# Raw weight tiles of the FFN in two sets of slots, with loads up to nine tiles ahead

## The chip, the cores and the metric

The kernel runs on one core of a Trainium2 chip. The metric is the time of one execution on the device, in microseconds (us). The engines are TensorE (PE in the profile; PEld is its weight load), VectorE (DVE), ScalarE (ACT), GpSimd (POOL) and SyncE (SP), which only issues DMAs here. Each takes its instructions from a queue of its own, in order, and waits on semaphores for the others.

## The reference

Two layers of an encoder trunk on x of 512 positions by 1024 channels, in float32. Each layer has two attention mixers (A: sparse, with an indexer and top-k; B: latent) with gates and projections, and then a channel mixer. The change sits in the weights of the channel mixer, called the FFN below:

```python
h = rms_norm(x, norm_ffn[l])
u = causal_dwconv(h @ w_up[l], conv_w[l], conv_b[l])      # w_up: 1024 x 5632, width 3
val, gat = u[..., :D_FF], u[..., D_FF:]                   # D_FF = 2816
x = x + (jax.nn.silu(gat) * val) @ w_down[l]              # w_down: 2816 x 1024
```

## The kernel before

All products are float32 made from three products of a shorter type: each operand is split in a high part (a cast on ScalarE) and a low part (the difference), and TensorE adds high by high, high by low and low by high.

The class `Weights` streams the weights from HBM as a list of tiles, 148 per layer, in the order in which TensorE uses them. The numbers of tiles below count from the start of layer 0. Tiles 0 to 59 belong to the mixers, the gates and the projections. The FFN has two parts. Part 1: up tiles `uv0`, `ug0` to `uv9`, `ug9` (value and gate columns; tiles 60 to 79), then 20 down tiles `dn` (80 to 99). Part 2: `uv10` to `ug21` (100 to 123), then 24 `dn` tiles (124 to 147). Layer 1 repeats this, 148 later.

A tile goes through these steps:

- `load` (L156): SP loads the raw tile `wr` (512 KB; 256 KB for `dn`). `wr` has four slots.
- `split` (L173, L191 for `dn`): ScalarE casts it to the high part `wh`.
- The low part `wl`: for `uv` and `ug`, `low_by_dma` lets ScalarE write the negated high part (L201), and POOL issues a DMA that adds the raw tile into it (L202). This accumulate DMA reads `wr`, so the slot is free when it has landed. For `dn`, VectorE subtracts (L196); so it does (L185) for an up tile right behind a `dn` tile.
- Before the split of a `dn` tile, `sums` (L213, L214, L215) makes its 4 blocks into 7 in place, for a product scheme with 7 products instead of 8. For the first four `dn` tiles of a part all three run on POOL; later, in part 1, L213 and L214 on VectorE and L215 on POOL; in part 2, L213 on VectorE and the others on POOL.

TensorE calls `get` for a tile. After its matmuls `ahead` runs: it splits the next three tiles and loads up to the sixth. Each up tile is 24 matmuls of 512 columns. Behind each up tile comes a conv: ScalarE L1365, then VectorE L1368 and L1369 from TensorE's bank; for a `ug` tile then silu (L357) and the product (L1386), and after every second pair `act_pair`, which makes the operands of the down tiles: L1342 to L1345, and the splits `b11`, `b21`, `t1`, `t3` (high parts on ScalarE, low parts at L303). A down tile is 21 matmuls of 256 columns (L1424), of which the first six read `b11`, `t1` and `t3`. The last three tiles of the kernel use `last_products` (L1495 to L1497).

Mixer A has pair tiles `P` of 128 x 1280, with three slots of their own (L1093, read by the transposes at L1052); they are not used in the FFN. The program is written in this order, and a list scheduler then sets each engine's queue.

Of the kernel before, what the change touches and what calls it, by code (L numbers as in the profile page):

```python
# [10 lines left out]
F32 = mybir.dt.float32  # L11
# [69 lines left out]
WMOD = 1  # L81
NEWT = 1
WB = [4, 4, 3]
N_SLOTS = 65
FS = 10
DNV = 1
# [42 lines left out]
W_COLS = max(n for _, _, n in PLAN)  # L129


class Weights:
# [18 lines left out]
    def load(self, i):  # L151
        if i >= len(self.seq) or i in self.raw:
            return
        n = self.seq[i][2]
        t = self.pool.tile([128, W_COLS], F32, name=f"wr{i}", tag="wr", bufs=WB[0])
        self.nc.sync.dma_start(t[:, :n], self.source(i, 0, n))  # L156
        self.raw[i] = t

    def split(self, i, lag=0):
# [4 lines left out]
        t = self.raw[i]  # L164
        h = self.pool.tile([128, W_COLS], F32R, name=f"wh{i}", tag="wh", bufs=WB[1])
        o = self.pool.tile([128, W_COLS], F32R, name=f"wl{i}", tag="wl", bufs=WB[1])
        name = self.seq[i][0]
# [36 lines left out]
    def sums(self, i, t):  # L204
# [3 lines left out]
        su = SU2 if self.seq[i][1] % 11 >= FS // 2 else SUMS  # L208
        if self.seq[i - WB[1]][0] != "dn":
            su = "012"  # L210
# [13 lines left out]
    def ahead(self):  # L224

        for j in range(1, WB[1]):
            self.split(self.at + j, 2)
        for j in range(WB[1], WB[1] + WB[0] - 1):
            self.load(self.at + j)
        if PRE and self.at + WB[1] < len(self.seq) and self.seq[self.at + WB[1]][0] == "dn":  # L230
            self.sums(self.at + WB[1], self.raw[self.at + WB[1]])
# [3 lines left out]
def trunk(ctx: ExitStack, tc: tile.TileContext, xT, wd, vecs, bias, rot_n, outT):  # L235
# [8 lines left out]
    def nm(s):  # L244
        uid[0] += 1
        return f"{s}_{uid[0]}"

    def slot(s, dt=F32):
        return sb.tile([128, 512], dt, name=nm(s), tag="slot", bufs=N_SLOTS)

# [118 lines left out]
    x0 = [slot("x") for _ in range(KD)]  # L369
    warm = sb.tile([128, 512], BF, name="warm", tag="slot", bufs=N_SLOTS)  # L370
    V.memset(warm, 0.0)
# [1257 lines left out]
```

## Time and profile before

| | |
|---|---|
| median of 3 runs (lowest to highest) | 1539.27 us (1538.85 to 1540.74) |
| profiled execution, and its span | 1542.47 us, 1540.8 us |
| granted clock | 1.00 |
| TensorE, TensorE's weight load | 1528.9 us (99%), 1337.1 us (87%) |
| VectorE, ScalarE, GpSimd | 1124.0 us (73%), 945.9 us (61%), 395.0 us (26%) |
| HBM | 141.06 MB read, 94 GB/s over the span |

The busy times are of one execution, and each row in the views names the engine, the line of the kernel, the tile that is written and those that are read. In the views of waits, an entry says who waited, at which line, for whom, and then the total in us, how often, and the longest. `SPq` is a load that waits in SP's queue for its slot.

### The profile page before, as it was taken

To read this page: it belongs to the slowest core of one execution; us is meant where nothing else is said; L and a number is where in the kernel's file an instruction comes from. 1 tells how busy PE (TensorE), PEld (TensorE's weight loads), DVE (VectorE), ACT (ScalarE), POOL (GpSimd) and SP (SyncE) were. 2 spreads that over 40 slices of the span, in tenths; PEclk is the share of its full clock that TensorE was granted. 3 is DMA by queue.
4 is the path that set the end of the run, shared out by engine and by line. 5 is a ranking of instruction groups with operands and counts; after the bars stand their busy time and mean duration, and the time that the engine had idled before them with its cause. 6 is when DMAs were issued, how large, how long until landed. Compare 5 with 4: busy or idle time off the path is not lost.

```text
span 1540.8 us, 23967 instructions
## 1 busy us (share of the span) xinstructions
PE 1528.9 (99%) x8666; PEld 1337.1 (87%) x8666; DVE 1124.0 (73%) x2303; ACT 945.9 (61%) x1553; POOL 395.0 (26%) x578
## 2 busy tenths in 40 slices
PE   9999999999999999999999999999999999999998
PEld 8887999888888898889998889998888888988898
DVE  7899988666476693547979999885574857845577
ACT  7756677773577536665557677686635765456642
POOL 2343012300012331125502520223001115311355
PEclk9999999999999999999999999999999999999999
DMA  7464124733478448873554641356435783588723
GB/s 245 104 160 122 46 92 110 186 120 119 127 189 190 103 117 219 191 178 96 151 165 112 166 99 56 103 135 173 131 99 144 177 190 95 152 197 195 176 77 109
DMA packets 73575, 216.29 MB, mean 140 GB/s; under 512 B 8432, under 2 KB 11504, under 8 KB 73456
## 3 DMA queue, kind: packets, MB, share of 16 engines
q1 hardware_dynamic: 54592, 149.08, 31.0%
q0 software_dynamic: 18432, 65.28, 22.6%
q8 instruction: 68, 1.11, 0.3%
q14 instruction: 51, 0.42, 0.1%
q10 hardware_dynamic: 432, 0.40, 0.1%
HBM read 141.06 MB, written 4.19 MB: 94 GB/s over the span
## 4 chain that ended last, share of the span: by engine, by line
PE 82%; DVE 12%; ACT 3%; issue 1%; POOL 0%; DMA 0%; DVEq 0%; ACTq 0%
PE D L516 35%; PE T L516 15%; PE D L539 6%; PE L L1424 5%; PE T L1424 4%; PE D L1424 3%; DVE sc L1021 2%; PE Y L1059 2%; DVE m L1014 2%; PE Y L1424 2%; PE T L1052 2%; PE L L516 2%; PE L L324 1%; PE L L323 1%; PE L L706 1%
## 5 line engine op out<-in xcount | busy, mean ns | idle before, releaser
L173 ACT CAST wh<-wr 128x1024 fp32r<-128x1024 f32 (+2 forms) x205 | 211.2, 1033 | 164.4 <-PE D L516 73.5
L202 POOL DMA_DIRECT2D wl<-wr x128 | 110.8, 877 | 633.0 <-ACT wl L201 604.4
L516 PE MATMUL D<-hxh,wh 128*128 128x512 f32 (+1 forms) x440 | 174.2, 396 | 0.0
L516 PE MATMUL D<-hxl,wh 128*128 128x512 f32 (+1 forms) x440 | 172.9, 393 | 0.0
L201 ACT ACTIVATE wl<-wr 128x1024 fp32r<-128x1024 f32 (+2 forms) x128 | 132.2, 1035 | 47.9 <-PE D L516 25.7
L191 ACT CAST wh<-wr 128x896 fp32r<-128x896 f32 x88 | 82.7, 941 | 103.8 <-POOL wr L215 69.6
L1093 POOL TENSOR_TENSOR P<-M,sel 128x128 f32<-128x128 f32 (+1 forms) x64 | 54.5, 907 | 272.9 <-DMA M<-in_bias_dram 239.3
L516 PE MATMUL D<-hxh,wl 128*128 128x512 f32 (+1 forms) x440 | 117.9, 393 | 0.0
L539 PE MATMUL D<-wh,hxh 128*128 128x256 f32 x384 | 113.8, 297 | 0.0
L196 DVE TENSOR_TENSOR wl<-wr,wh 128x896 fp32r<-128x896 f32 x88 | 103.8, 1181 | 8.2 <-ACT wh L191 3.1
L215 POOL TENSOR_TENSOR wr<-wr 128x256 f32<-128x256 f32 x88 | 93.8, 1068 | 60.8 <-DVE wr L214 48.3
L539 PE MATMUL D<-wl,hxh 128*128 128x256 f32 x384 | 109.3, 285 | 0.0
L539 PE MATMUL D<-wh,hxl 128*128 128x256 f32 x384 | 108.4, 283 | 0.0
L185 DVE TENSOR_TENSOR wl<-wr,wh 128x1024 fp32r<-128x1024 f32 x77 | 95.4, 1245 | 6.6 <-ACT wh L173 5.6
L516 PE MATMUL D<-hrl,wh 128*128 128x512 f32 x256 | 99.6, 389 | 0.0
L516 PE MATMUL D<-hrh,wh 128*128 128x512 f32 x256 | 99.6, 389 | 0.0
L516 PE MATMUL T<-hrh,wh 128*128 128x512 f32 x256 | 99.6, 389 | 0.0
L516 PE MATMUL T<-hrl,wh 128*128 128x512 f32 x256 | 99.6, 389 | 0.0
L516 PEld LDWEIGHTS D<-hxh,wh 128*128 128x128 f32 x440 | 82.9, 188 | 13.4 <-DVE gb L680 0.2
L516 PEld LDWEIGHTS D<-hxl,wh 128*128 128x128 f32 x440 | 82.9, 188 | 12.7
L516 PEld LDWEIGHTS D<-hxh,wl 128*128 128x128 f32 x440 | 80.2, 188 | 14.0
L1368 DVE SCALAR_TENSOR_TENSOR c<-T,vec,c 128x511 f32<-128x511 f32 x32 | 23.9, 748 | 89.1 <-ACT c L1365 89.1
(454 smaller groups left out, 4577.2 us busy)
## 6 DMA issues: line engine op xcount, KB each, us to landing
wr<-in_wd_dram SPq DMA_DIRECT2D x197, 512.0 KB, 3.7
wl<-wr POOLq DMA_DIRECT2D x120, 512.0 KB, 5.3
wr<-in_wd_dram SPq DMA_DIRECT2D x88, 256.0 KB, 2.6
x<-in_xT_dram SPq DMA_DIRECT2D x16, 256.0 KB, 4.8
M<-in_bias_dram SPq DMA_DIRECT2D x16, 256.0 KB, 4.0
wr<-in_wd_dram SPq DMA_DIRECT2D x7, 384.0 KB, 3.3
kah<-kah SPq DMA_DIRECT2D x16, 128.0 KB, 4.5
kal<-kal SPq DMA_DIRECT2D x16, 128.0 KB, 3.7
```

The costliest lines, as they stand in the source:

```text
L173: ins = self.nc.scalar.copy(h[:, :n], t[:, :n])
L185: eng.tensor_tensor(out=o[:, c], in0=t[:, c], in1=h[:, c].bitcast(F32), op=OP.subtract)
L191: self.nc.scalar.copy(h[:, :896], t[:, 128:1024])
L196: self.later(lag, lambda: self.nc.vector.tensor_tensor(out=o[:, :896], in0=t[:, 128:1024], in1=h[:, :896].bitcast(F32), op=OP.subtract))
L201: self.nc.scalar.activation(o, t, AF.Copy, scale=-1.0)
L202: self.nc.gpsimd.dma_start(o.bitcast(F32), t, accum_op=OP.add)
L215: g(2)(out=b[:, 6:8], in0=b[:, 0:3:2], in1=b[:, 3:6:2], op=OP.add)
L516: mm(p[:, t0:], lhsT=w, rhs=x[:, t0:], start=n == 0, stop=n == len(seq) - 1, skip_group_check=True)
L539: mm(pp[b][:, t, :], lhsT=x, rhs=w, start=n == 0 and half == 0 and t == 0, stop=n == 11 and half == 1, skip_group_check=True)
L1014: ins = V.max(out=m8[i], in_=st["sc"][i][:, :128 * (i + 1)])
L1093: G.tensor_tensor(out=P[:, P0[i]:P0[i] + w], in0=M[:, 512 - w:512], in1=sel[:, SEL0[i]:SEL0[i] + w], op=OP.add)
L1424: mm(p, lhsT=w, rhs=x, start=b0, stop=b1, skip_group_check=True)
```

## The change

FFN tiles whose number leaves 1, 3 or 5 when divided by 7 are loaded into the three slots of mixer A's pair tiles (tag `P`), the others into the four slots of `wr`. In the FFN a raw slot is so used again by the tile seven later, where it was four. `ahead` loads up to the ninth tile instead of the sixth, as far as these are FFN tiles. Splits still look three tiles ahead; the `sums` of a `dn` tile four ahead are still asked for at the end of `ahead`. Lines below the first edit move by 3 to 5 in `Weights` (L156 is L161 after, L202 is L207, L213 is L218), and by 7 behind it (L1368 is L1375, L1424 is L1431).

```diff
--- before.py
+++ after.py
@@ -81,6 +81,8 @@
 WMOD = 1
 NEWT = 1
 WB = [4, 4, 3]
+FFN = ('uv', 'ug', 'dn')
+SPARE = (1, 3, 5)
 N_SLOTS = 65
 FS = 10
 DNV = 1
@@ -151,8 +153,11 @@
     def load(self, i):
         if i >= len(self.seq) or i in self.raw:
             return
-        n = self.seq[i][2]
-        t = self.pool.tile([128, W_COLS], F32, name=f"wr{i}", tag="wr", bufs=WB[0])
+        name, _, n, _ = self.seq[i]
+        if name in FFN and i % (WB[0] + WB[2]) in SPARE:
+            t = self.pool.tile([128, 1280], F32, name=f"wr{i}", tag="P", bufs=WB[2])
+        else:
+            t = self.pool.tile([128, W_COLS], F32, name=f"wr{i}", tag="wr", bufs=WB[0])
         self.nc.sync.dma_start(t[:, :n], self.source(i, 0, n))
         self.raw[i] = t
 
@@ -225,7 +230,9 @@
 
         for j in range(1, WB[1]):
             self.split(self.at + j, 2)
-        for j in range(WB[1], WB[1] + WB[0] - 1):
+        for j in range(WB[1], WB[1] + WB[0] - 1 + WB[2]):
+            if j >= WB[1] + WB[0] - 1 and not (self.at + j < len(self.seq) and self.seq[self.at + j][0] in FFN):
+                break
             self.load(self.at + j)
         if PRE and self.at + WB[1] < len(self.seq) and self.seq[self.at + WB[1]][0] == "dn":
             self.sums(self.at + WB[1], self.raw[self.at + WB[1]])
```

TensorE's queue is the same in both. The queues of VectorE and POOL differ near the ends of the up tiles and in the down tiles. In the two fences that follow, from POOL at the end of layer 0's part 1, `t` is `act_pair`'s first subtract (L1342, L1349 after), and the rows of 128x1024 are accumulate DMAs. Before, `wl_5490`, `wl_5550`, `wl_5586`, `wl_5624` belong to tiles 75, 76, 77, 78 (`ug7`, `uv8`, `ug8`, `uv9`), and `wr_5590`, `wr_5628` to tiles 80, 81:

```order
L1342 TENSOR_TENSOR t_5512<-c_5420 128x256
L202 DMA wl_5490<-wr_5380 128x1024
L202 DMA wl_5550<-wr_5418 128x1024
L202 DMA wl_5586<-wr_5458 128x1024
L213 TENSOR_TENSOR wr_5590<-wr_5590 128x128
L214 TENSOR_TENSOR wr_5590<-wr_5590 128x128
L215 TENSOR_TENSOR wr_5590<-wr_5590 128x256
L202 DMA wl_5624<-wr_5494 128x1024
L213 TENSOR_TENSOR wr_5628<-wr_5628 128x128
L214 TENSOR_TENSOR wr_5628<-wr_5628 128x128
L215 TENSOR_TENSOR wr_5628<-wr_5628 128x256
L1342 TENSOR_TENSOR t_5685<-c_5592 128x256
```

After, the same accumulates write `wl_5496`, `wl_5556`, `wl_5592`, `wl_5630`, and `wr_5464`, `wr_5500`, `wr_5560`, `wr_5596` are tiles 80 to 83:

```order
L207 DMA wl_5496<-wr_5230 128x1024
L218 TENSOR_TENSOR wr_5500<-wr_5500 128x128
L219 TENSOR_TENSOR wr_5500<-wr_5500 128x128
L220 TENSOR_TENSOR wr_5500<-wr_5500 128x256
L218 TENSOR_TENSOR wr_5560<-wr_5560 128x128
L219 TENSOR_TENSOR wr_5560<-wr_5560 128x128
L220 TENSOR_TENSOR wr_5560<-wr_5560 128x256
L207 DMA wl_5556<-wr_5276 128x1024
L207 DMA wl_5592<-wr_5320 128x1024
L218 TENSOR_TENSOR wr_5596<-wr_5596 128x128
L219 TENSOR_TENSOR wr_5596<-wr_5596 128x128
L220 TENSOR_TENSOR wr_5596<-wr_5596 128x256
```

The sums of 80 (just above these rows), 81 and 82 have moved ahead of accumulate 76, and those of 83 ahead of accumulate 78.

VectorE at the same place, before: `c<-D` is the conv of `uv7`, `c<-T` that of `ug7`, and L1386 the product of the two:

```order
L303 TENSOR_TENSOR b11l_5519<-c_5592,b11h_5518 128x256
L1368 SCALAR_TENSOR_TENSOR c_5630<-D_5594,vec,c_5630 128x511
L1369 SCALAR_TENSOR_TENSOR c_5630<-D_5594,vec,c_5630 128x510
L1368 SCALAR_TENSOR_TENSOR c_5669<-T_5632,vec,c_5669 128x511
L1369 SCALAR_TENSOR_TENSOR c_5669<-T_5632,vec,c_5669 128x510
L1386 TENSOR_TENSOR c_5669<-c_5669,c_5630 128x512
```

After, `wr_5634` is tile 84 and `wr_5670` tile 85:

```order
L310 TENSOR_TENSOR b11l_5525<-c_5598,b11h_5524 128x256
L218 TENSOR_TENSOR wr_5634<-wr_5634 128x128
L1375 SCALAR_TENSOR_TENSOR c_5636<-D_5600,vec,c_5636 128x511
L219 TENSOR_TENSOR wr_5634<-wr_5634 128x128
L1376 SCALAR_TENSOR_TENSOR c_5636<-D_5600,vec,c_5636 128x510
L218 TENSOR_TENSOR wr_5670<-wr_5670 128x128
L1375 SCALAR_TENSOR_TENSOR c_5675<-T_5638,vec,c_5675 128x511
L219 TENSOR_TENSOR wr_5670<-wr_5670 128x128
L1376 SCALAR_TENSOR_TENSOR c_5675<-T_5638,vec,c_5675 128x510
L1393 TENSOR_TENSOR c_5675<-c_5675,c_5636 128x512
```

The first two sums of tiles 84 and 85 (L218, L219), which before stood behind the convs of `uv8` and `ug8`, now stand ahead of and between those of `uv7` and `ug7`.

## The prediction

> **What bounds the kernel now.** I read the page first, then the list of waits, then TensorE's chain.
>
> ```profile
> PE 1528.9 (99%) x8666; PEld 1337.1 (87%) x8666; DVE 1124.0 (73%) x2303; ACT 945.9 (61%) x1553; POOL 395.0 (26%) x578
> ...
> PE D L1497 <- DVE wl L196: 1.5, 1, 1.5
> PE T L376 <- DVE warm L371: 1.2, 1, 1.2
> ...
> SPq L156 <- DMA wl<-wr: 745.1, 128, 14.9
> ...
> 508.95 5.44 PE D L516 x24
> ...
> 538.26 0.72 PE D L1424 x6
> ...
> 540.78 0.98 PE D L1424 x6
> ```
>
> TensorE is busy for 99% of the span, and its order does not change. In the FFN the list shows one wait of it, the 1.5 us at the kernel's end. SP's weight loads do wait, 745.1 us in total behind the accumulate DMAs that free a raw slot, but no TensorE wait follows from that: more raw slots remove a wait that costs nothing. So the question is how the new order of the other queues changes the times at which TensorE gets its operands. The last two rows show where nothing is spare: the first down tiles of layer 0's part 1 (TensorE goes over from `ug9` to `dn` at 530.7). Six matmuls take 0.72 us elsewhere and 0.98 us at 540.78. They read `b11h`, `b11l`, `t1h`, `t1l`, `t3h`, `t3l`, and `t3l` is the last thing that VectorE writes before them:
>
> ```profile
> 510.74 0.75 DVE L1368 SCALAR_TENSOR_TENSOR c<-T,vec,c 128x511 f32<-128x511 f32 x1 [3.90 <-ACT c L1365]
> ...
> 513.03 0.69 DVE L1386 TENSOR_TENSOR c<-c,c 128x512 f32<-128x512 f32 x1 [0.76 <-ACT c L357]
> ...
> 540.64 0.68 DVE L303 TENSOR_TENSOR t3l<-t,t3h 128x512 fp32r<-128x512 f32 x1
> ```
>
> `t3l` is ready at 541.32; its matmul is the sixth, due at 540.78 + 5 x 0.12 = 541.38. Whatever delays VectorE's chain from the conv of `ug7` (510.74) to `t3l` stalls TensorE one for one, once VectorE's idle time in that stretch is used up.
>
> **The new chain of slots.** The loads go out earlier, and the scheduler sets the first down tiles' `sums` earlier in POOL's and VectorE's queues. Both queues run in order. Before, accumulate DMA 75 (`ug7`) to 78 (`uv9`) ran ahead of or between sums whose tiles were long loaded:
>
> ```profile
> 488.58 0.87 POOL L202 DMA_DIRECT2D wl<-wr  x1 [3.81 <-ACT wl L201]
> 495.32 0.86 POOL L202 DMA_DIRECT2D wl<-wr  x1 [5.86 <-ACT wl L201]
> ...
> 505.19 0.46 POOL L213 TENSOR_TENSOR wr<-wr 128x128 f32<-128x128 f32 x1 [4.87 <-DMA wr<-in_wd_dram]
> 505.73 0.47 POOL L214 TENSOR_TENSOR wr<-wr 128x128 f32<-128x128 f32 x1
> 506.27 0.74 POOL L215 TENSOR_TENSOR wr<-wr 128x256 f32<-128x256 f32 x1
> 506.95 0.86 POOL L202 DMA_DIRECT2D wl<-wr  x1
> ```
>
> In the changed order POOL does: accumulate 75, sums of 81 and 82, accumulates 76 and 77, sums of 83, accumulate 78. Tile i's load takes the slot of tile i-7 and waits for that tile's accumulate. So the queues form one serial chain: accumulate 75 lands, load 82, sums of 82, accumulate 76 lands, load 83, sums of 83, accumulate 78 lands, load 85, and then VectorE's L213 of tile 85, which now stands in VectorE's queue ahead of the conv of `ug7`. Its prices:
>
> ```profile
> DMA to landing us min/median/max: 4.4/5.0/6.0
> ...
> wr<-in_wd_dram SPq DMA_DIRECT2D x3, 256.0 KB, 4.3
> ...
> DMA to landing us min/median/max: 2.5/2.6/4.6
> ...
> 536.12 0.29 DVE L213 TENSOR_TENSOR wr<-wr 128x128 f32<-128x128 f32 x1 [0.93 <-DMA wr<-in_wd_dram]
> ```
>
> The first row is the accumulate DMA from 484 to 515 us; the second the median 256 KB load in the same stretch, where accumulates are in flight; the third the 256 KB load from 500 to 545 us, mostly alone.
>
> - Three accumulates: 3 x 5.0 = 15.0 us (13.2 to 18.0).
> - Three loads. Load 82 meets no accumulate, since 76 stands behind its sums: 2.6. Load 83 meets accumulate 77, issued right after 76: 4.3. For load 85 it is open whether accumulate 79 is out already: I take 3.4. Together 10.3 (7.8 to 12.9).
> - Two sets of sums on POOL, 505.19 to 507.01: 2 x 1.8 = 3.6. One L213 on VectorE: 0.3.
> - Start. Sums of 80 and a subtract now stand ahead of accumulate 75. Tile 80 waits for accumulate 73, about two tiles (2 x 5.44) before 488.58, so 477.7; plus 5.0, a load of 2.6 to 4.3, 1.8 and 0.7, that ends between 487.8 and 489.5. I take a delay of 0.7 (0 to 2).
>
> The conv of `ug7` so starts 15.0 + 10.3 + 3.6 + 0.3 + 0.7 = 29.9 us after 488.58, where it started 22.2 after it: 7.7 late (2.7 with every low end, 14.6 with every high one).
>
> **The Trainium skill on the accumulate DMA.** The trace has 4.4 to 6.0 us for 512 KB. The Trainium skill, page "DMA: Bandwidth & Descriptors", section "Anatomy of one DMA — SWDGE (gpsimd) path", gives a fit of 2.0 us plus bytes over 436 GB/s for a DMA that GpSimd issues, an estimate of 3.2 us here; by it the chain would be 3 x 1.8 = 5.4 us shorter, 24.5 us long, and nothing below would stall. The trace does not agree, and I stay with it.
>
> **What the delay costs at the four places.** The same code runs at the end of both parts' up tiles, in both layers. I ask VectorE's busy time from the conv of the like `ug` tile to `t3l`:
>
> ```profile
> 510.74:541.32 30.58, 24.79 (x41) 1.00 0.35 86
> 691.98:722.57 30.59, 24.64 (x38) 1.00 0.35 91
> 1274.46:1303.41 28.95, 23.73 (x41) 1.00 0.42 105
> 1455.44:1487.88 32.44, 26.51 (x38) 1.00 0.32 81
> ...
> 724.53 1.20 PE L L1424 x10
> ...
> 1304.50 0.72 PE D L1424 x6
> ...
> 1488.00 1.20 PE L L1424 x10
> ```
>
> Columns are the stretch, its length, VectorE's busy time and its instructions. When VectorE is late, its idle time shrinks to what the data force: two waits of 0.76 for silu, 1.5. The new order also puts about 0.9 us more of L213/L214 into part 1's stretch and 0.6 into part 2's. So `t3l` comes at least 27.2, 26.7, 26.1 and 28.6 us after the conv. TensorE needs it 30.6, 33.1, 30.6 and 33.2 us after the conv's old start (the row's start plus 0.6). Late by 7.7, the stalls are 4.3, 1.3, 3.2 and 3.1: 11.9 us. With every low end of the chain the delay is 2.7 and there is no stall anywhere; with every high end about 39. Accumulates are slower near layer 0's part 2 and layer 1's part 1, which I leave out, since VectorE's busy time holds some contention that a spread-out order would lose.
>
> **The other parts of the change.** TensorE, and the matmuls' count and bytes: nothing changes. ScalarE: the same casts, not earlier, because `split` still looks three tiles ahead; cost zero under TensorE's 5.44 us per tile. SP issues the same loads in another order. Its queue is in order too: a load into one of mixer A's pair slots waits for the last reader, a transpose, and the loads behind it wait as well:
>
> ```profile
> 336.89 0.27 PE L1052 MATMUL T<-ident,P 128*128 128x128 f32 x1
> ...
> 340.17 0.33 SPq L156 DMA_DIRECT2D wr<-in_wd_dram  x1
> ```
>
> The last of the three loads (tile 66) now stands just ahead of the load that was issued at 340.17; its slot is free at 337.2, so that load and the x loads behind it lose nothing. If the slot were freed later, x would be late by the excess.
>
> The tail gains. The last wait of TensorE is for the last low part:
>
> ```profile
> 1521.84 0.69 DVE L213 TENSOR_TENSOR wr<-wr 128x128 f32<-128x128 f32 x1 [0.59 <-DMA wr<-in_wd_dram]
> ...
> 1523.90 0.29 DVE L213 TENSOR_TENSOR wr<-wr 128x128 f32<-128x128 f32 x1 [0.37 <-DMA wr<-in_wd_dram]
> ...
> 1529.62 1.09 DVE L196 TENSOR_TENSOR wl<-wr,wh 128x896 fp32r<-128x896 f32 x1
> ```
>
> VectorE waited for loads at 1521.84 and 1523.90, and the last low part ended at 1530.71, 1.5 us late. With down tiles loaded seven slots ahead these load waits and the last sums leave that stretch: between 0 (other work fills it) and 1.5. I take 1.5, since 0.96 us of load waits and 0.98 of sums are in the two rows alone.
>
> **Sum.** 11.9 - 1.5 = +10.4. The profiled execution took 1542.47 us, 3.2 above the runs' median of 1539.27, with the same waits; I put the difference on the median: 1549.7.
>
> **Rivals.**
>
> - *Short latencies.* Every accumulate lands in about 4.5 us and every load in 2.6, as the low ends of the rows allow. Load 85 lands before about 514, VectorE takes up the delay in its idle time, and only the tail counts: 1537.8. The point that decides is a conv delay of about 3.4 us. For it: spreading the loads may thin out collisions. Against it: all must be near their minimum, and at the median accumulates alone cost 15.0. This is the case on the other side, and it is what the rule quoted above would give.
> - *Nothing happens.* TensorE waits for no load in the FFN, so earlier loads alone change nothing: 1539.3. It needs the moved sums to be harmless, and the tail's last low part to stay bound by VectorE's other work.
> - *Long latencies.* Accumulates at 6.0, loads at 4.3: delay 10 to 14, stalls of 6 to 11 per place, 1560 to 1577.
> - *SP blocked.* A pair slot freed later than its load's turn delays x or gate loads by a few us: 1541 to 1545. Against it stand the rows at 336.89 and 340.17.
>
> **How the numbers follow.** Stalls near my sum 0.68, short latencies 0.16, nothing 0.06, long latencies 0.07, SP 0.03. About 0.2% (3.1 us) is what a measurement can tell from no change. Slower by more: the long case, most of SP's, and the sum's case but for 0.02 in which the stalls only just exceed the tail's gain: 0.76. Within: short latencies, nothing, and that rest: 0.22. Faster by over 0.2% would need 3.1 us, and TensorE's waits in the FFN before total under 2: 0.02. The range reaches from the short case, 1537.5, to 1560, which takes stalls of 5.6 per place; the long case above it is the part left out. The likeliest case alone is 1543 to 1558.
>
> **What would show it.** Right: waits of TensorE at L1431 for `t3l` (L310) near 545, 730, 1310 and 1495, of some us each; VectorE waiting at L218 for a load just ahead of the conv, POOL at L218 for loads between accumulates; SP's wait for accumulate DMAs still large, or larger near 490 to 515; no 1.5 us wait at L1504. Wrong: load 85 landing before 514, or VectorE keeping up with `t3l` because its queue on the chip holds enough idle time; or a tail wait that stays.

## The result, and the profile after

The changed kernel takes 1561.64 us (median of 6 runs, 1555.47 to 1567.5), the kernel before beside it 1539.51 (1538.85 to 1540.74). The ratio is 1.0142, 95% interval 1.0114 to 1.0169: 22.1 us slower. The forecast was 1549.7 with a range up to 1560, so the sign and the place were right, and half the size was missing. The profiled execution took 1565.16 us, span 1563.1, at a mean granted clock of 0.993 where the kernel before had 1.000. Over the six executions this clock was 0.992 to 0.997, and the longer the time, the lower it was: 0.997 at 1555.47 and 1557.81 us, 0.992 at 1567.5.

The page's first row and TensorE's list of waits, after. An entry of the list says who waited, for whom, and then the total in us, how often and the longest:

```profile
PE 1539.5 (98%) x8666; PEld 1345.9 (86%) x8666; DVE 1117.3 (71%) x2303; ACT 943.5 (60%) x1553; POOL 393.6 (25%) x578
```

```profile
PE D L1431 <- DVE b11l L310: 4.2, 2, 2.1
PE L L1431 <- DVE t1l L310: 3.0, 2, 1.5
PE L L1431 <- DVE b11l L310: 2.4, 2, 1.6
PE D L1431 <- ACT b11h L309: 2.3, 2, 1.6
PE T L383 <- DVE warm L378: 1.2, 1, 1.2
...
PE D L1431 <- DVE t1l L310: 1.2, 2, 0.7
```

Two things are to be seen. New waits at L1431, all for the operands of the last pair, come to 13.1 us. And TensorE's busy time has grown by 10.6 us (1528.9 before) with the same 8666 matmuls: the matmuls themselves became slower. Four stretches of 20 us around the four ends show both; columns are the stretch, its length, TensorE's busy time and matmuls, the mean granted clock, and the DMAs' share and rate:

```profile
540.00:560.00 20.00, 15.86 (x104) 0.83 0.37 106
725.00:745.00 20.00, 17.64 (x130) 0.91 0.31 92
1310.00:1330.00 20.00, 16.43 (x110) 0.83 0.32 93
1500.00:1520.00 20.00, 16.83 (x124) 0.91 0.29 87
```

Idle time is 4.1, 2.4, 3.6 and 3.2 us, 13.2 in all. The clock below 1.00 costs 20 x (0.17 + 0.09 + 0.17 + 0.09) = 10.4 us, within 0.2 us the growth in busy time. Single microseconds at the first end show that the clock goes to 0.50 and comes back:

```profile
544.00:545.00 1.00, 0.14 (x1) 0.98 0.00 0
...
546.00:547.00 1.00, 0.94 (x3) 0.50 0.46 166
...
551.00:552.00 1.00, 1.00 (x7) 0.61 0.32 119
552.00:553.00 1.00, 1.00 (x11) 1.00 0.00 0
```

The chain there shows the same in the matmuls (start, length, matmuls):

```profile
546.06 1.19 PE D L1431 x3
547.25 1.71 PE T L1431 x8
...
552.28 0.48 PE Y L1431 x4
```

Eight matmuls take 1.71 us, 0.21 each; behind 552 they take 0.12 again.

The chain of slots can be followed on POOL and then on VectorE (start, length, line, tile, and in brackets the idle time before and what ended it):

```profile
491.12 0.88 POOL L207 DMA_DIRECT2D wl<-wr  x1
...
498.24 0.46 POOL L218 TENSOR_TENSOR wr<-wr 128x128 f32<-128x128 f32 x1 [3.98 <-DMA wr<-in_wd_dram]
...
500.00 1.76 POOL L207 DMA_DIRECT2D wl<-wr  x2
509.73 0.46 POOL L218 TENSOR_TENSOR wr<-wr 128x128 f32<-128x128 f32 x1 [7.96 <-DMA wr<-in_wd_dram]
...
511.49 0.86 POOL L207 DMA_DIRECT2D wl<-wr  x1
```

```profile
510.47 0.40 DVE L218 TENSOR_TENSOR wr<-wr 128x128 f32<-128x128 f32 x1 [6.85 <-DMA wr<-in_wd_dram]
...
519.81 0.29 DVE L218 TENSOR_TENSOR wr<-wr 128x128 f32<-128x128 f32 x1 [7.42 <-DMA wr<-in_wd_dram]
520.02 0.74 DVE L1375 SCALAR_TENSOR_TENSOR c<-T,vec,c 128x511 f32<-128x511 f32 x1
...
545.92 0.68 DVE L310 TENSOR_TENSOR t3l<-t,t3h 128x512 fp32r<-128x512 f32 x1
```

Accumulate 75 is issued at 491.12, the sums of 82 wait for their load until 498.24, accumulate 76 goes out at 500.00, the sums of 83 start at 509.73, accumulate 78 at 511.49. VectorE stands 7.42 us at L218 for load 85, the conv of `ug7` starts at 520.02 and `t3l` ends at 546.60, where it was 541.32. SP's wait behind accumulate DMAs, which the change was to relieve, is as large as before:

```profile
SPq L161 <- DMA wl<-wr: 753.8, 128, 14.0
...
SPq L161 <- PE T L1059: 11.6, 4, 4.6
```

The second row is new: loads that wait for the transposes of mixer A to free a pair slot. No TensorE wait follows from it.

### The profile page after: what moved, and what is told of

It reads as the page before. It is cut to its first block, busy times and chain, and to the rows that moved or that the text cites. A ratio compares the mean times of both kernels' runs of the same rounds, so it can differ in the third digit from the quotient of the medians.

```text
span 1563.1 us, 24025 instructions
## 1 busy us (share of the span) xinstructions
PE 1539.5 (98%) x8666; PEld 1345.9 (86%) x8666; DVE 1117.3 (71%) x2303; ACT 943.5 (60%) x1553; POOL 393.6 (25%) x578
## 4 chain that ended last, share of the span: by engine, by line
PE 73%; DVE 15%; DMA 6%; ACT 3%; issue 2%; POOL 1%; DVEq 0%; SPq 0%; POOLq 0%; ACTq 0%
PE D L523 32%; PE T L523 11%; PE D L546 7%; PE L L1431 4%; DMA wr<-in_wd_dram 3%; PE T L1431 3%; PE D L1431 2%; DVE sc L1028 2%; PE Y L1066 2%; DVE m L1021 2%; PE T L1059 2%; DMA wl<-wr 2%; PE Y L1431 2%; DVE wl L201 2%; PE L L331 1%
## 5 line engine op out<-in xcount | busy, mean ns | idle before, releaser
L207 POOL DMA_DIRECT2D wl<-wr x128 | 111.1, 883 | 593.9 <-ACT wl L206 570.3
L220 POOL TENSOR_TENSOR wr<-wr 128x256 f32<-128x256 f32 x88 | 95.6, 1091 | 77.4 <-DVE wr L219 56.4
L364 ACT ACTIVATE c<-c 128x512 f32<-128x512 f32 x44 | 27.8, 632 | 114.6 <-DVE c L1376 114.6
```

What stands on the lines that cost most here:

```text
L207: self.nc.gpsimd.dma_start(o.bitcast(F32), t, accum_op=OP.add)
L220: g(2)(out=b[:, 6:8], in0=b[:, 0:3:2], in1=b[:, 3:6:2], op=OP.add)
```

## The experiments

### Slots without the earlier loads

```diff
-        for j in range(WB[1], WB[1] + WB[0] - 1 + WB[2]):
+        for j in range(WB[1], WB[1] + WB[0] - 1):
```

> The changed kernel with the loads issued six tiles ahead as before; only the second set of slots stays. The queues of POOL and VectorE come out in the changed kernel's order. Serial-chain theory (sums ahead of accumulate DMAs on POOL, L218 ahead of the convs on VectorE, late t3l, then a halved TensorE clock): nothing is undone, 1555 to 1567 us, TensorE waits near 13 us in four places. Rival, that the loads' depth and their traffic cost the time: near 1539 us.

Measured: 1562.67 us, ratio 1.014 (1.0118 to 1.0162), the changed kernel's time, as expected; the conv of `ug7` starts at 519.71. Loads requested six tiles ahead do the same as nine; the second set of slots alone moves the sums in the queues. The depth of the loads is no part of the cause.

### Holding back the sums on VectorE, on POOL, and on both

Sums are ordered behind the last conv that was traced before them (VectorE), or behind the last accumulate DMA (POOL). `ops` are the three sums. It is an order in the queue, not a wait:

```diff
+        for j, ins in enumerate(ops):
+            last = self.acc if str(j) in su else self.tap
+            if last is not None and ("G" if str(j) in su else "V") in BEHIND:
+                self.behind(ins, last)
...
+        self.acc = self.nc.gpsimd.dma_start(o.bitcast(F32), t, accum_op=OP.add)
...
+                W.tap = V.scalar_tensor_tensor(c[:, 2:512], u[:, 0:510], w(0), c[:, 2:512], op0=OP.mult, op1=OP.add)
```

VectorE alone (`BEHIND = 'V'`):

> The changed kernel, but VectorE's sums (L218, L219) are held behind the conv that was traced last before them, so no L218 stands ahead of the convs of uv7 and ug7. POOL's order stays changed. Serial-chain theory: the convs come at their old times, t3l is ready in time at all four ends, no wait of TensorE there and no halved clock, tail gain kept: 1537 to 1541 us. Rival, that the accumulates' lateness or the traffic itself makes TensorE wait: 1550 us or more, with waits for wl at L523 or for wh.

Measured: 1540.15 us, ratio 0.9998 (0.9988 to 1.0008). From its POOL and VectorE rows (lines lie 2 to 7 further than in the changed kernel: L220 is L218 there, L209 is L207, L316 is L310, L1382 is L1375):

```profile
509.61 0.46 POOL L220 TENSOR_TENSOR wr<-wr 128x128 f32<-128x128 f32 x1 [7.74 <-DMA wr<-in_wd_dram]
...
511.36 0.88 POOL L209 DMA_DIRECT2D wl<-wr  x1
```

```profile
510.64 0.75 DVE L1382 SCALAR_TENSOR_TENSOR c<-T,vec,c 128x511 f32<-128x511 f32 x1 [3.91 <-ACT c L1379]
...
540.21 0.68 DVE L316 TENSOR_TENSOR t3l<-t,t3h 128x512 fp32r<-128x512 f32 x1
```

```profile
540.00:560.00 20.00, 20.00 (x169) 1.00 0.31 91
```

POOL's serial chain is still there, accumulate 78 just as late (511.36), with the same seven slots and traffic. But VectorE no longer stands behind it: the conv of `ug7` starts at 510.64, `t3l` is there at 540.89, and TensorE has neither idle time nor a slow clock here or at the other three ends. The new wait of SP for the pair slots is there too (11.5 us) and costs nothing. All 22 us hang on the L218s that stand ahead of the convs.

POOL alone (`BEHIND = 'G'`):

> The changed kernel, but POOL's sums of the first four down tiles are held behind the last accumulate DMA that was traced before them. VectorE's order stays changed. Serial-chain theory: accumulates 75 to 79 are issued at the old times (about 488, 495, 499, 505, 510), load 85 lands at 513 to 516 and the conv of ug7 is 3 to 5 us late in place of 9; TensorE waits 0 to 2 us at layer 0's part 1 and less elsewhere: 1538 to 1545 us. Rival, that the extra VectorE work ahead of t3l alone makes the stalls: near 1560 us.

Measured: 1557.1 us, ratio 1.0111 (1.0094 to 1.0127). My expectation missed; the time is near the rival's. The accumulates did go out at the old times, yet:

```profile
503.82 0.86 POOL L209 DMA_DIRECT2D wl<-wr  x1 [4.58 <-ACT wl L208]
```

```profile
515.21 1.92 DVE L220 TENSOR_TENSOR wr<-wr 128x128 f32<-128x128 f32 x1 [4.97 <-DMA wr<-in_wd_dram]
517.05 0.74 DVE L1382 SCALAR_TENSOR_TENSOR c<-T,vec,c 128x511 f32<-128x511 f32 x1
```

This execution runs 1.1 us earlier than the others here, so the conv at 517.05 is 7.4 us late, against 9.3 in the changed kernel. Accumulate 78, issued at 503.82, landed only at 510.56, with loads in flight; load 85 took another 4.3; and L220 itself took 1.92 us instead of 0.29, beside POOL's sums. At the other three ends this last part is the largest. Layer 0's part 2, and then the same subtract in layer 1's part 1 and part 2 (in the last one place earlier in the queue, ahead of the value tile's conv):

```profile
697.78 5.39 DVE L220 TENSOR_TENSOR wr<-wr 128x128 f32<-128x128 f32 x1 [3.39 <-DMA wr<-in_wd_dram]
703.10 0.74 DVE L1382 SCALAR_TENSOR_TENSOR c<-T,vec,c 128x511 f32<-128x511 f32 x1
```

```profile
1282.88 4.95 DVE L220 TENSOR_TENSOR wr<-wr 128x128 f32<-128x128 f32 x1 [3.42 <-DMA wr<-in_wd_dram]
...
1466.64 4.97 DVE L220 TENSOR_TENSOR wr<-wr 128x128 f32<-128x128 f32 x1 [8.72 <-DMA wr<-in_wd_dram]
```

The loads had landed by then. Held back, POOL's sums run in one row without a gap (696.19 to 703.02 at layer 0's part 2), and at all four ends the subtract ended 0.15 to 0.17 us behind that row. Without it the conv at 703.10 would have started at about 698.0, an estimate of 2 us late, since ScalarE's part of it ended at 695.96. So a good part of the delay in this run is a new wait, made by holding the sums back, and the run doesn't settle what POOL's order is worth in the changed kernel. The time is 4.5 us under the changed kernel's, and the intervals just overlap.

Both (`BEHIND = 'VG'`):

> The changed kernel with both: VectorE's sums behind the convs and POOL's sums behind the accumulates. Serial-chain theory: all four stalls gone and the tail's 1.5 us gained, 1537 to 1539 us, 0.1% below the kernel before. Rival, that seven slots and earlier loads cost through traffic: above 1545 us.

Measured: 1540.28 us, ratio 0.9998 (0.9988 to 1.0008), as VectorE alone. No stall, and no gain of 0.1% either, so the time is above my range.

### Filling TensorE's wait

20 matmuls of zeros ahead of the awaited down tile, at each of the four ends; `n` counts the down groups of a part:

```diff
+                for _ in range(FILL if n == 0 and kp == pairs[-1] else 0):
+                    tc.keep_in_program_order(mm(region(banks, 0, False), lhsT=zero[:, :128], rhs=zero, start=False,
+                                                stop=False, skip_group_check=True))
```

> The changed kernel, but TensorE gets 20 more matmuls of 256 columns with zeros (2.4 us, added to a bank without effect) just ahead of the down tile at which it waits, at all four ends. They lie inside the waits of 4.2, 2.3, 3.6 and 3.1 us. Theory that idle time halves TensorE's clock: the matmuls behind the wait run at full speed at least where 2.4 us cover nearly all of it, clock rows of 0.50 vanish in two to four places, 1549 to 1555 us. Rival, that the slow matmuls have another cause (late operands, contention of their reads): the clock rows of 0.50 stay and the time is that of the changed kernel, 1556 us or more.

Measured: 1558.79 us, ratio 1.0113 (1.0097 to 1.0128), above my bound and where the rival had it. Its stretches:

```profile
540.00:560.00 20.00, 17.63 (x123) 0.83 0.32 92
725.00:745.00 20.00, 17.70 (x145) 1.00 0.31 80
1310.00:1330.00 20.00, 20.00 (x169) 1.00 0.28 80
```

Where the fill covered the wait (1310, and the fourth end as well), or left 2.3 us (725), the clock stayed; where it left 2.4 us, it fell all the same. So the clock rows speak for the theory and the time for the rival. The time decides nothing here, because the waits differ from the changed kernel's: at 725 the fill (20 x 0.11) and what is left of the wait (2.3) come to 4.5 us, where the wait was 2.4, and two of the four executions had a clock of 1.000 and took 1554.02 and 1558.6 us. A second one therefore fills the whole wait, 40 matmuls at the ends of part 1 and 28 at those of part 2 (`FILL = {0: 40, 10: 28}`):

> The changed kernel with 40 matmuls of zeros (4.8 us) ahead of the awaited down tile at the two ends of part 1 and 28 (3.4 us) at those of part 2, as long as the whole waits of the changed kernel. Clock theory: TensorE is never idle there, so no row of granted clock 0.50; the cost is the fill alone, 2 x 4.8 + 2 x 3.4 = 16.4 us, less the tail's 1.5 or so: 1553 to 1556 us, though more matmuls are run than in the changed kernel (1556 to 1567). Rival, slow matmuls for another reason: about 10 us more, 1563 us or above.

Measured: 1556.93 us, ratio 1.0108 (1.0089 to 1.0127).

```profile
PE 1543.6 (99%) x8802; PEld 1350.5 (87%) x8802; DVE 1113.2 (72%) x2304; ACT 943.6 (61%) x1553; POOL 395.7 (25%) x578
```

```profile
540.00:560.00 20.00, 19.66 (x165) 1.00 0.32 88
725.00:745.00 20.00, 20.00 (x172) 1.00 0.33 90
```

The operands come as late as before, but TensorE is hardly idle (0.3 us at the first end), and no stretch of the execution is below 1.00. Its busy time is 14.7 us over that of the kernel before: the 136 added matmuls at 0.11 us. The median lies 4.7 us under the changed kernel's although more is computed (the intervals overlap a little). The time is 1 us or so over what I expected; one wait of 1.4 us in mixer A of this execution may be part of that.

### Waits of chosen length in the kernel before

VectorE writes `t3l` of the last pair again, some times over; `EXTRA` has the number of further writes by layer and pair:

```diff
+EXTRA = {(0, 4): 1, (0, 10): 3, (1, 4): 4, (1, 10): 2}
...
+                for _ in range(EXTRA.get((l, kp), 0) if n1 == "t3" else 0):
+                    later(2, lambda o=o, src=src, h=h: V.tensor_tensor(out=o, in0=src, in1=h.bitcast(F32),
+                                                                       op=OP.subtract))
```

> The kernel before, where t3l of the last pair is written again 1, 3, 4 and 2 times by VectorE at the four ends (layer 0 parts 1 and 2, layer 1 parts 1 and 2), so that TensorE waits by estimate 1.6, 1.7, 3.4 and 2.7 us there. Clock theory: waits over 2 us are followed by 3 to 7 us of granted clock 0.50, shorter ones are not (the 1.5 us wait of the kernel before had none): about +9 us of waits and +4 to 7 us of slow matmuls. Rival: clock rows stay 1.00, +9 us in all.

Measured, one execution: 1551.35 us. The waits came out shorter than I had estimated:

```profile
540.00:560.00 20.00, 18.64 (x155) 1.00 0.38 105
720.00:740.00 20.00, 18.51 (x155) 1.00 0.36 106
1310.00:1330.00 20.00, 18.07 (x139) 0.91 0.29 87
1490.00:1510.00 20.00, 19.33 (x161) 1.00 0.36 106
```

With none of the change's slots or loads, one wait of 1.9 us at the third end is followed by a clock of 0.91, and waits of 1.4, 1.5 and 0.7 us are not. The same execution has a second fall, in mixer A of layer 1, far from the added writes, behind one wait of 2.0 us:

```profile
1047.10 0.45 PE L1060 MATMUL Y<-ptl,va 128*128 128x256 f32 x1 [2.01 <-DVE ptl L304]
```

```profile
1040.00:1060.00 20.00, 17.99 (x84) 0.91 0.68 168
```

The four waits (5.5 us), this one (2.0) and two slow stretches of 1.8 us come to 11.1 us, and the execution is 11.2 us over the median of the kernel before beside it (1540.2).

The second allocation, `EXTRA = {(0, 4): 4, (0, 10): 5, (1, 4): 2, (1, 10): 1}`:

> The same with 4, 5, 2 and 1 further writes: waits by estimate 4 to 5, 4, 1.5 and 1 us. Clock theory: granted clock 0.50 for some us at the first two ends, none at the last two. Rival: no row under 1.00 behind any of them, or behind all.

Measured, one execution: 1543.95 us. Again the waits were shorter than meant, 1.6 us at each of the first two ends and none at the others, because VectorE had more idle time to give:

```profile
540.00:560.00 20.00, 18.45 (x154) 1.00 0.37 101
725.00:745.00 20.00, 18.38 (x154) 1.00 0.40 119
```

No row is under 1.00, so this run adds to the short waits and does not test the long ones.

### The tail

The other slots and the deeper loads for the last 20 weight tiles alone, in the kernel before:

```diff
+TAIL_AT = 276
...
-        if name in FFN and i % (WB[0] + WB[2]) in SPARE:
+        if i >= TAIL_AT and i % (WB[0] + WB[2]) in SPARE:
```

> The kernel before, with the other three slots and loads up to nine ahead for the last 20 weight tiles alone (from tile 276, the down tiles of the last part but the first four). Theory: the only gain in the change is the tail's wait for the last low part, 1.5 us, with no stall: 1537.5 to 1538.5 us, and no wait at L1497's line. Rival, that VectorE's work bounds the last low part: 1539.3 us.

Measured: 1541.17 us, ratio 1.0005 (0.9997 to 1.0014): no gain. My expectation missed, and the rival's no change holds. TensorE's wait for the last low part is gone from the list, though. Hence a second profile of the kernel before, with no edit:

> The kernel before, profiled once more, to see whether the tail's 1.5 us wait of TensorE for the last low part (L196) is there in each execution. If it is: the same wait at L1497, 1.3 to 1.6 us, and the gain of 1.5 us that the profiles of the kernels with held-back sums show has to be hidden by something in the timed runs. Rival: it comes and goes with the loads' latencies, and was in the first profile by chance.

Measured: 1539.02 us, span 1537.3. Its list of TensorE's waits begins so, and has no L1497:

```profile
PE T L376 <- DVE warm L371: 1.2, 1, 1.2
PE L L834 <- DVE vb L303: 1.2, 3, 0.6
PE L L323 <- ACT rl L1001: 0.8, 2, 0.5
```

So the wait of 1.5 us is not in every execution of the kernel before: the first profile, 3.2 us above the median, has it, and the second does not.

## Why the prediction was right or wrong, point by point

- **Bound and place: right.** In the FFN TensorE waits for no load, before or after. All new waits are at L1431 for the last pair's operands, at the four ends named.
- **The chain of slots: right in its links.** From the old issue of accumulate 75 (488.58) to the conv of `ug7` it took 31.4 us; the sum had 29.9. The start was 2.5 late (forecast 0.7) and the accumulates were quick (4.4, 4.5 and 4.4 for 75, 76 and 78, forecast 5.0 each), load 83 took 5.1 us.
- **VectorE ahead of the convs: shown.** With the same late accumulates but L218 behind the convs the whole loss is gone. The prediction put as much weight on POOL's order. Holding POOL's sums back alone left 17 of 22 us, but with a new wait of up to 5 us beside POOL's row, so the share of POOL's order stays open.
- **The waits: right in sum, with some luck.** Forecast 4.3, 1.3, 3.2 and 3.1, in all 11.9; idle time measured 4.1, 2.4, 3.6 and 3.2, in all 13.2. But the convs were 9.5, 8.5, 8.6 and 8.0 us late (counted from ScalarE's part of the conv), not 7.7, and with these delays the prediction's own working gives 6.1, 2.1, 4.1 and 3.4, in all 15.7. At the first end VectorE made up 4.0 us (the 9.3 by which its conv was late, less the 5.3 of `t3l`), not 3.4. What was wrong in detail: VectorE's lateness arrives not only at `t3l` but already at `b11h`, `b11l` and `t1l`, so that a wait comes in two or three pieces.
- **The step that failed: "stalls TensorE one for one".** The sum priced a wait of TensorE at its length and the slower matmuls behind it at nothing. That holds in these runs only up to some 1.6 us. Behind the longer waits the matmuls ran at half speed for 3.5 to 7 us, which added 10.4 us to 13.2. The profile before had no wait long enough to show it, and I did not bound it. The six timed executions agree: their clocks of 0.997 to 0.992 are worth about 5 to 12 us each, and with that taken off each comes to 1551 to 1555 us, near the forecast's sum without the tail.
- **The tail's gain: wrong.** The term of 1.5 us was read from one execution of the kernel before, and the second does not have it. No kernel with the other slots in the tail was faster for it. Without the term the forecast's own sum is 1551.2.
- **Sum with the measured terms:** 13.2 + 10.4 = 23.6, against 22.1 in the medians and 26.1 between the profiled execution (1565.16) and the second one of the kernel before (1539.02). Of the remaining 2.5, some 1.9 lie in TensorE's busy time, which is 1527.2 in that second profile against 1528.9 in the first; where they arise is not shown.
- **Rivals.** The long latencies had 1560 and above, and the time falls there, but not for their reason: accumulates were at their low end and stalls at 2 to 4 us, not 6 to 11. SP did wait 11.6 us for pair slots, without a TensorE wait behind it.

## What to carry to other kernels

More buffers do not help where the consumer never waits, and they can hurt: instructions that the scheduler now sees as ready are placed earlier in an in-order queue, and when the data are late in fact, everything behind them is late. Look at what stands behind each moved instruction, and hold it back by an order edge if it isn't urgent; then look at what the held-back work now runs beside. Price a stall of a busy TensorE at its length plus the slow matmuls behind it, and take a small gain only from a wait that more than one execution shows.

## What the runs showed of the hardware

TensorE's granted clock can fall to half behind a short pause. The table has, for the 20 us around each of the four ends, the idle time in us and the mean granted clock:

| | layer 0, part 1 | layer 0, part 2 | layer 1, part 1 | layer 1, part 2 |
|---|---|---|---|---|
| changed kernel | 4.1, 0.83 | 2.4, 0.91 | 3.6, 0.83 | 3.2, 0.91 |
| slots only | 4.1, 0.83 | 2.3, 0.91 | 2.9, 0.91 | 3.0, 0.91 |
| POOL held back | 2.9, 0.91 | 1.2, 1.00 | 2.7, 1.00 | 2.7, 0.83 |
| first fill | 2.4, 0.83 | 2.3, 1.00 | none | none |
| chosen waits, first | 1.4, 1.00 | 1.5, 1.00 | 1.9, 0.91 | 0.7, 1.00 |
| chosen waits, second | 1.6, 1.00 | 1.6, 1.00 | none | none |

In these 20 stretches with a pause, idle time of up to 1.6 us was never followed by a clock under 1.00 (6 stretches), 1.9 to 2.7 us was in 5 of 7, and 2.9 to 4.1 us always (7 of 7). Part of the idle time can lie behind the fall. The loss is not gradual: means of 0.91 and 0.83 over 20 us are about 3.5 and 7 us at half speed, with nothing between.

The Trainium skill, page "TensorE: Matmul & The Clock Gate", section "Part 1: The HAM clock gate (the "warmup" mystery)", has the clock at half after an idle window of about 3.4 us and back after a busy one, with a window that runs freely. The lengths of the slow stretches agree with one or two such windows. But no pause here was that long without a break: a single one of 1.9 us was enough, so was one of 2.0 us in mixer A of the same execution, and the longest piece in any was 2.1 us. A window need not be fully idle, it seems; how idle it must be, these runs don't settle.

An instruction of VectorE can stand still beside a row of POOL's instructions. With POOL's sums held back, a subtract of 128x128 that takes 0.29 us elsewhere took 1.92, 5.39, 4.95 and 4.97 us and ended just behind POOL's row each time. With both held back it is a product of 128x512 at each of the four ends (L1400, 4.88 us instead of 0.69), and there VectorE had the time to spare.
